# Experts' products issued by quarters of a matrix instead of whole matrices, and the first expert's low parts made on VectorE after the routing

## The chip, the cores and the metric

The kernel is one program on 1 core of a Trainium2 chip. Its time is device microseconds (us) of that core, given as the median of the runs. The engines are named as the profile names them: PE is TensorE (PEld its weight loads), DVE is VectorE, ACT is ScalarE, POOL is GpSimd and SP is SyncE, whose queue issues the large transfers.

## The reference, cut to what matters

The whole program is two blocks on 512 tokens of width 1024. The first is a state space mixer, an MLP, a sparse attention and another MLP. The second is an attention block followed by a mixture of 32 experts, and the change concerns this last layer alone. Each token goes to its 4 best experts. Every expert has three matrices of 1024 x 1024 in f32:

```python
logits = (h @ router_w + router_b).astype(jnp.float32)
top_logit, top_e = lax.top_k(logits, TOP_K)
top_w = jax.nn.softmax(top_logit, axis=-1)
...
gate = jnp.minimum(xe @ w_gate[e] + b_gate[e], SWIGLU_LIMIT)
up = jnp.clip(xe @ w_up[e] + b_up[e], -SWIGLU_LIMIT, SWIGLU_LIMIT)
act = (up + 1) * (gate * jax.nn.sigmoid(SWIGLU_ALPHA * gate))
return act @ w_down[e] + b_down[e]
```

A matrix is 4 MB, and all the experts' matrices together are 32 x 3 x 4 MB = 384 MB (of 1.0486 million bytes each), which have to be read once.

## The kernel before

**Routing.** `route` works out each token's weights, counts the tokens of each expert, sorts the experts by that count into ranks (`kr`, `gt`, `perm`), and stores the expert's number for each rank in `permi` and each token's place within its expert in `place`. `first` does the same ahead of that for rank 0, which is always the expert with number 0, and gathers its rows (`xy<-hx,gi`), so that this expert can start without the ranks. `route` also splits the three bias tables into a high and a low part (`b_gate`, `b_up`, `b_down`).

**Sizes of experts.** By rank an expert is computed in one of four ways. Ranks 1 to 3 (`HEAVY`) take two blocks of rows: 128 and 128 for rank 1, 128 and 64 for ranks 2 and 3. Ranks 0 and 4 to 10 take one block of 128 rows. Ranks 11 to 21 (`LIGHT`) take 64 rows and ranks 22 to 31 (`TINY`) take 32. The first eleven are called large below, the other 21 small.

**A quarter.** A matrix is read in four transfers of 1 MB on SP's queue (`fetch`, the tile `raw`). RAWS = 8 buffers hold them, and an issue waits until its buffer has been read out. For a large expert ACT rounds each half of a quarter to `wh` (L1772) and DVE subtracts that from `raw` to get `wl` (L1774), after which `raw` is free; then PE makes three products of 512 columns for each half and each half of the output (`mm3`, L170 to L172), 12 in a quarter. SPLITS buffers hold `wh`, as many `wl`. For expert 0 the low parts of the first two quarters are made on POOL, by the condition in L1774. For a small expert PE reads `raw` itself in f32 (L1804, `lac<-raw,xtf`), two or four column groups side by side, and `raw` is free once PE is through.

**The order.** `units` writes out a list of matrices (rank, t), t = 0 for gate, 1 for up, 2 for down. After expert 0, two matrices of small experts stand ahead of each matrix of a large one. `run` walks the list. In it `product` does all four quarters of a matrix, `after` the element-wise work behind it (L1860 to L1867), `act` transposes the gated rows for the third matrix (L1738, L1727), `table` finds an expert's rows (L1697, L1700), `gather` fetches them on POOL (L1713), and `start` transposes them. Tables are asked for five matrices ahead, gathers four. The function `ahead` splits the first two quarters of a large matrix before its turn. Within this order a scheduler moves single instructions, so that the matmuls of neighbouring pieces mix a little. The result of an expert is added to the output by an indirect DMA (L1890, `out_dram<-xy,si`).

Of the kernel before, what the change touches and what calls it, by code (L numbers as in the profile page):

```python
# [9 lines left out]
F32 = mybir.dt.float32  # L10
# [8 lines left out]
P = 128  # L19
NB = 4  # L20
# [1333 lines left out]
SPLITS = 5  # L1354
# [12 lines left out]
def units():  # L1367
# [25 lines left out]
class Moe:  # L1393
# [122 lines left out]
    def route(self):  # L1516
# [7 lines left out]
        self.bias = []  # L1524
        for n in ("b_gate_2", "b_up_2", "b_down_2"):
            raw = self.wp.tile([P, D], F32, name="bw", tag="wh")[:, :512]
            for i in range(4):
                nc.gpsimd.dma_start(raw[NE * i:NE * i + NE], a[n][0][:, i // 2 * 512:i // 2 * 512 + 512])
            x = bp.tile([P, 512], F32R, name=n)
            S.copy(x, raw)  # L1530
            for i in (1, 3):
                s = slice(NE * i, NE * i + NE)
                V.tensor_tensor(x[s], raw[s], x[s].bitcast(F32), op=OP.subtract)
            self.bias.append(x)
# [75 lines left out]
        V.tensor_copy(self.cnt, o)  # L1610

# [7 lines left out]
    def first(self, w4):  # L1619
# [24 lines left out]
        x0 = self.gather(gi)  # L1644
# [10 lines left out]
        self.xt0 = self.tiles(x0)  # L1655
# [33 lines left out]
    def table(self, r):  # L1689
# [5 lines left out]
        for i, slot in enumerate(todo):  # L1695
            oh = self.tp.tile([P, NB, P], F32R, name="ohs", bufs=1)
# [46 lines left out]
    def expert(self, e, xts, slots, es, out_rows, G=1):  # L1743
# [8 lines left out]
        early = bool(raws)  # L1752
# [13 lines left out]
        def split(t, c):  # L1766
            if (t, c) not in parts:
                raw = get(t, c)
                parts[t, c] = []
                for j in range(2):  # L1770
# [3 lines left out]
                    (G_ if early and t == 0 and c < 2 else V).tensor_tensor(wl, raw[:, j], wh.bitcast(F32), op=OP.subtract)  # L1774
                    parts[t, c].append((wh, wl))
            return parts[t, c]

        def ahead(t):
            if G == 1:
                for c in range(2):  # L1780
                    split(t, c)

        def act(t):

            if t == 2:
                st[2] = [self.tiles(u, G) for u in st["g"]]

        def grouped(t, mid):
            N, m = D // G, P // G
            ps = self.kk.ps.tile([P, 512], F32, name="lac", bufs=2)[:, :N]  # L1790
            b = self.bias[t]
            if G == 2:
                T.matmul(ps, pick[:, 0], b, start=True, stop=False)
            else:
                for i in range(2):
                    T.matmul(ps, pick[:, i], b[:, 256 * i:256 * i + 256], start=i == 0, stop=False)
# [371 lines left out]
```

## Time and profile before

| what | value |
|---|---|
| time, median of 3 runs | 2981.14 us (2977.97 to 2982.78) |
| the profiled execution's own time | 2984.59 us |
| its span in the trace | 2982.8 us, 38289 instructions |
| busy share of the span | PE 90%, PEld 67%, DVE 59%, ACT 40%, POOL 8% |
| moved between HBM and the core | 574.49 MB read, 21.53 MB written, 200 GB/s over the span |

Times in the rows below count from the start of the span. The experts' stage begins near 1841 us and lasts to the end. A busy PE in these rows is not PE at its peak, since the ends of matmuls are modelled; how fast it really goes is seen from the starts of successive matmuls.

### The profile page before, as it was taken

The page shows a single profiled execution, that of the slowest core. Times are in us where ns is not written, and L with a number is a line of the kernel's source. Part 1 is how long each engine was busy: PE and PEld are TensorE (multiplying, and loading weights), DVE is VectorE, ACT ScalarE, POOL GpSimd, SP SyncE. Part 2 cuts the span into 40 slices and gives each one's busy share as a digit, 9 for nine tenths or more (in the row PEclk, how much of TensorE's full clock was granted, in tenths as well). Part 3 has the DMA queues.
Part 4 walks back from the last instruction along what each step waited for, and adds up shares of the span by engine and source line. Part 5 has one row for each costly group of instructions (what it writes and reads, how often), then busy time and mean ns, then how long its engine had stood idle before and what let it go on. Part 6 is the DMA issues. An engine that isn't in the chain of part 4 may idle for free. (4 is left out here: it accounts for less than half of the span.)

```text
span 2982.8 us, 38289 instructions
## 1 busy us (share of the span) xinstructions
PE 2677.6 (90%) x14182; PEld 1996.0 (67%) x14182; DVE 1770.5 (59%) x3419; ACT 1191.8 (40%) x2208; POOL 245.2 (8%) x229
## 2 busy tenths in 40 slices
PE   5599999987999999899998997999989989988986
PEld 3488777886778888788888775556455455444553
DVE  6967565578874444589777558444444444444443
ACT  5353232454863333366655434332233232333232
POOL 3000000142000000200000002110110110110010
PEclk9799999998999999999999997999989999999997
DMA  3024454321023333211122555998999998999997
GB/s 116 15 99 176 150 197 156 94 60 54 29 93 127 96 96 99 93 50 41 53 60 72 181 198 203 385 361 358 349 353 363 342 357 353 350 359 376 381 406 295
DMA packets 193999, 595.95 MB, mean 200 GB/s; under 512 B 34960, under 2 KB 106056, under 8 KB 141320
## 3 DMA queue, kind: packets, MB, share of 16 engines
q1 hardware_dynamic: 179744, 564.33, 50.8%
q0 software_dynamic: 8752, 28.58, 3.4%
q8 instruction: 113, 1.85, 0.2%
q10 hardware_dynamic: 5312, 0.54, 0.1%
q14 instruction: 78, 0.64, 0.1%
HBM read 574.49 MB, written 21.53 MB: 200 GB/s over the span
## 5 line engine op out<-in xcount | busy, mean ns | idle before, releaser
L1804 PE MATMUL lac<-raw,xtf 128*32 128x256 f32 (+1 forms) x2976 | 378.6, 461 | 6.4 <-DMA raw<-in_w_down_dram 3.8
L152 DVE TENSOR_TENSOR wl<-wr,wh 128x1024 fp32r<-128x1024 f32 (+2 forms) x222 | 262.3, 1187 | 177.6 <-ACT wh L150 173.8
L150 ACT CAST wh<-wr 128x1024 fp32r<-128x1024 f32 (+2 forms) x228 | 228.8, 1008 | 295.4 <-PE acc L172 162.0
L1774 DVE TENSOR_TENSOR wl<-raw,wh 128x1024 fp32r<-128x1024 f32 x260 | 303.7, 1219 | 36.3 <-ACT wh L1772 35.2
L171 PE MATMUL wide<-wl,xth 128*128 128x512 f32 x576 | 259.8, 451 | 30.8 <-DVE wl L1774 30.6
L170 PE MATMUL wide<-wh,xth 128*128 128x512 f32 x576 | 256.1, 446 | 33.7 <-ACT wh L1772 32.4
L1772 ACT CAST wh<-raw 128x1024 fp32r<-128x1024 f32 x264 | 260.8, 1045 | 62.5 <-PE wide L172 37.0
L1804 PEld LDWEIGHTS lac<-raw,xtf 128*32 128x32 f32 (+1 forms) x2976 | 126.3, 119 | 193.8 <-issue 155.2
L170 PE MATMUL mm<-wh,xh 128*128 128x384 f32 (+2 forms) x664 | 230.1, 346 | 27.0 <-ACT gate L1264 12.8
L172 PE MATMUL wide<-wh,xtl 128*128 128x512 f32 x576 | 250.2, 434 | 0.0
L171 PE MATMUL mm<-wl,xh 128*128 128x384 f32 (+2 forms) x664 | 222.7, 335 | 3.1 <-DVE wl L152 2.9
L172 PE MATMUL mm<-wh,xl 128*128 128x384 f32 (+2 forms) x664 | 222.5, 335 | 1.2 <-DVE xl L166 1.2
L171 PE MATMUL acc<-wl,ffh 128*128 128x512 f32 x512 | 199.3, 389 | 0.7 <-DVE wl L152 0.7
L172 PE MATMUL acc<-wh,ffl 128*128 128x512 f32 x512 | 199.4, 390 | 0.0
L170 PE MATMUL acc<-wh,ffh 128*128 128x512 f32 x512 | 198.6, 390 | 0.0
L171 PEld LDWEIGHTS wide<-wl,xth 128*128 128x128 f32 x576 | 122.2, 212 | 99.4 <-DVE wl L1774 56.2
L170 PEld LDWEIGHTS wide<-wh,xth 128*128 128x128 f32 x576 | 121.3, 211 | 88.9 <-ACT wh L1772 46.6
L170 PEld LDWEIGHTS mm<-wh,xh 128*128 128x128 f32 x664 | 129.0, 194 | 44.1 <-ACT gate L1264 17.1
L172 PEld LDWEIGHTS wide<-wh,xtl 128*128 128x128 f32 x576 | 122.2, 212 | 34.7 <-issue 11.4
L171 PEld LDWEIGHTS mm<-wl,xh 128*128 128x128 f32 x664 | 129.0, 194 | 9.8 <-DVE wl L152 5.3
L172 PEld LDWEIGHTS mm<-wh,xl 128*128 128x128 f32 x664 | 129.2, 195 | 7.0 <-DVE xl L166 1.9
L1890 POOL DMA_INDIRECT out_dram<-xy,si x35 | 65.4, 1867 | 662.1 <-DVE xy L1889 482.2
(641 smaller groups left out, 5417.7 us busy)
## 6 DMA issues: line engine op xcount, KB each, us to landing
raw<-in_w_gate_dram SPq DMA_DIRECT2D x128, 1024.0 KB, 8.5
raw<-in_w_up_dram SPq DMA_DIRECT2D x128, 1024.0 KB, 11.4
raw<-in_w_down_dram SPq DMA_DIRECT2D x128, 1024.0 KB, 7.3
wr<-in_mlp_w_dram SPq DMA_DIRECT2D x128, 512.0 KB, 3.7
adaraw<-in_w_ada_dram SPq DMA_DIRECT2D x12, 2048.0 KB, 7.5
wr<-in_w_in_dram SPq DMA_DIRECT2D x16, 512.0 KB, 3.9
wr<-in_att_w_out_dram SPq DMA_DIRECT2D x12, 512.0 KB, 3.9
wr<-in_w_in_dram SPq DMA_DIRECT2D x48, 128.0 KB, 2.4
```

The source lines that it names most:

```text
L150: nc.scalar.copy(hi, raw)
L152: (eng or nc.vector).tensor_tensor(lo, raw, hi.bitcast(F32), op=OP.subtract)
L170: mmul(ps, ah, bh, start=first, stop=False)
L171: mmul(ps, ah, bl, start=False, stop=False)
L172: mmul(ps, al, bh, start=False, stop=last)
L1772: S.copy(wh, raw[:, j])
L1774: (G_ if early and t == 0 and c < 2 else V).tensor_tensor(wl, raw[:, j], wh.bitcast(F32), op=OP.subtract)
L1804: T.matmul(ps[m * g:m * g + m], x, raw[:, j, N * g:N * g + N], start=False, stop=c == 3 and j == 1)
L1890: G_.indirect_dma_start(out=out_rows, out_offset=bass.IndirectOffsetOnAxis(ap=si[:rows], axis=0), in_=y, in_offset=None, bounds_check=511, ...
```

## The change

The list holds quarters (rank, t, c) now (`steps`): expert 0's first six quarters stand alone, and from then on two quarters of small experts mostly follow each quarter of a large one. A large matrix's splits run one quarter ahead of its products. The hooks for table, gather and transposes sit at fixed distances in quarters: a table 16 ahead of an expert's first quarter, the gather 10, the transposes 8 for a large expert and 3 for a small one. The gated rows of a large expert are transposed two places ahead of its third matrix, which is behind two small quarters. The list of which expert follows which is unchanged, and so is the arithmetic but for the place of the bias products, which stand in a matrix's last quarter now. POOL no longer makes low parts. The rows of expert 0 and the bias tables are prepared at the end of `route`. SPLITS goes from 5 to 4, and the one-hot tile `ohs` has two buffers. The special early fetch of expert 0's third matrix is gone.

```diff
-SPLITS = 5
+SPLITS = 4
...
-    lane = iter(lane)
-    order = [(0, 0), (0, 1), next(lane), (0, 2)]
-    for u in [(r, t) for r in big[1:] for t in range(3)]:
-        order += [next(lane), next(lane), u]
+    lane = iter([(*u, c) for u in lane for c in range(4)])
+    order = []
+    for r in big:
+        gaps = [0] * 6 + [2, 2, 2, 2, 2, 0] if r == 0 else [2] * 7 + [4, 2, 2, 2, 0]
+        for (t, c), n in zip([(t, c) for t in range(3) for c in range(4)], gaps):
+            order += [(r, t, c)] + [x for _, x in zip(range(n), lane)]
     return order + list(lane)
...
         self.cnt = cp.tile([P, NE], F32, name="cnt")
         V.tensor_copy(self.cnt, o)
+        self.xt0 = self.tiles(self.x0)
+        for n, raw in zip(("b_gate_2", "b_up_2", "b_down_2"), raws):
+            x = bp.tile([P, 512], F32R, name=n)
+            S.copy(x, raw)
+            for i in (1, 3):
+                s = slice(NE * i, NE * i + NE)
+                V.tensor_tensor(x[s], raw[s], x[s].bitcast(F32), op=OP.subtract)
+            self.bias.append(x)
...
         def split(t, c):
-            if (t, c) not in parts:
+            if G == 1 and (t, c) not in parts:
                 raw = get(t, c)
...
-                    (G_ if early and t == 0 and c < 2 else V).tensor_tensor(wl, raw[:, j], wh.bitcast(F32), op=OP.subtract)
+                    V.tensor_tensor(wl, raw[:, j], wh.bitcast(F32), op=OP.subtract)
...
-            if early and t == 0:
-                raws.update(((2, c), self.fetch(e, (2, c))) for c in range(4))
...
+        n = 0
+        whole = [u for u in todo if groups(u[0]) == 1]
+        for p, (r, t, c) in enumerate(todo):
+            if r and t == c == 0:
+                n += 1
+                a = max(p - 16, n)
+                b = max(p - 10, a + 2)
+                at(a, table, r)
+                at(b, gather, r)
+                at(max(p - (8 if groups(r) == 1 else 3), b + 2), start, r)
+            if t == 2 and c == 0:
+                at(p - 2 if groups(r) == 1 else p - 3, lambda r: ex[r][1](), r)
         start(0)
...
+        ex[0][0](0, 0)
+        k = 0
+        for p, (r, t, c) in enumerate(todo):
+            for f in hooks.get(p, []):
+                f()
+            if groups(r) == 1 and (k := k + 1) < len(whole):
+                q, tq, cq = whole[k]
+                ex[q][0](tq, cq)
+            ex[r][2](t, c)
```

Where instructions stand is decided by the list and by the scheduler, so three places are shown as the built programs have them. The first is VectorE in the routing, from the one-hot rows of `first` (`w`, `ax`, weights of rank 0) and of all experts (`one`, `sw`) on. Before:

```order
L1550 TENSOR_TENSOR one<-one,w_16423 128x128
L1650 TENSOR_TENSOR ax_16441<-w_16464,ax_16441 128x4
L1551 TENSOR_REDUCE sw<-one 128x32
L1533 TENSOR_TENSOR b_up_16410<-bw,b_up_16410 32x512 x2
L1666 COPY sv_16474<-tr 128x4
L1551 TENSOR_REDUCE sw<-one 128x32
```

And after the change, from a few rows further up to the same reductions:

```order
L1553 SCALAR_TENSOR_TENSOR kc<-mm,c_keyc 128x1
L1778 TENSOR_TENSOR wl<-raw,wh 128x1024
L1647 TENSOR_SCALAR gi_16447<-tr 128x1
L1654 TENSOR_REDUCE w_16452<-w_16451 128x4
L1548 TENSOR_TENSOR one<-one,w_16411 128x128
L1655 CAST ax_16429<-w_16452 128x4
L1548 TENSOR_TENSOR one<-one,w_16411 128x128
L1656 TENSOR_TENSOR ax_16429<-w_16452,ax_16429 128x4
L1549 TENSOR_REDUCE sw<-one 128x32 x2
L1671 COPY sv_16462<-tr 128x4
```

The pair of `b_up` rows has moved from among the reductions to a place behind `perm`, and a first low part `wl` of expert 0, which was POOL's, stands on VectorE ahead of `gi`.

The second place is SyncE's queue behind the routing, where `TENSOR_LOAD permi` reads an expert's number and `ISA` are the checks on it. Before, three stretches of it:

```order
L1513 DMA hx<-nrm 128x1024 x4
L1429 DMA raw<-in_w_down_dram 128x2048 x2
L1904 TENSOR_LOAD permi
L1904 ISA x2
...
L1429 DMA raw<-in_w_gate_dram 128x2048
```

And after, where ten loads stand between the rows that are shown:

```order
L1516 DMA hx<-nrm 128x1024 x4
L1898 TENSOR_LOAD permi
L1898 ISA x2
...
L1432 ISA
L1432 DMA raw<-in_w_gate_dram 128x2048
L1432 ISA
L1432 DMA raw<-in_w_gate_dram 128x2048
L1432 DMA raw<-in_w_down_dram 128x2048
```

The two transfers of expert 0's third matrix that stood ahead of the loads are now mixed, one by one, with those of the small experts' quarters, and all of them are behind ten loads.

The third place is PE in the middle of the stage, around the transposes of the gated rows (`tr<-c_ident,gm`) of a large expert of one block, with tiny experts beside it. Before (24 rows of products of a large expert, L170 to L172, are left out in the middle):

```order
L1804 MATMUL lac<-raw,xtf 64x512 x12
L1793 MATMUL lac<-b_down_16419,pick 128x512
L1727 MATMUL tr<-c_ident,gl 128x128 x4
...
L1804 MATMUL lac<-raw,xtf 32x256 x16
L1738 MATMUL tr<-c_ident,gm 128x128 x8
L1727 MATMUL tr<-c_ident,xg 128x128 x2
```

And after the change:

```order
L172 MATMUL wide<-wh,xtl 128x512
L1796 MATMUL lac<-raw,xtf 32x256 x8
L1790 MATMUL lac<-b_up_16583,pick 128x256 x2
L1743 MATMUL tr<-c_ident,gm 128x128 x8
L1743 MATMUL tr<-c_ident,xy 128x128 x2
L170 MATMUL wide<-wh,xth 128x512
```

Where three quarters of a small expert (`x12`), two of a large one and two small ones stood in runs, single small quarters (`x8` of 256 columns, `x4` of 512) alternate with single large ones; between the large products and the transposes of `gm` stands one small quarter where there were two.

## Rows read from the trace of the kernel before

**Rows 1.** The page's 40 slices of the span, 74.6 us each: clock and transfers.

```profile
PEclk9799999998999999999999997999989999999997
...
GB/s 116 15 99 176 150 197 156 94 60 54 29 93 127 96 96 99 93 50 41 53 60 72 181 198 203 385 361 358 349 353 363 342 357 353 350 359 376 381 406 295
```

**Rows 2.** Busy times, clock and transfers by stretch; the first line names the columns.

```profile
core 0: us, PE busy (x) PEld busy (x) DVE busy (x) ACT busy (x) POOL busy (x), PEclk, DMA share, GB/s
1841.00:1900.00 59.00, 59.00 (x260) 34.67 (x259) 37.94 (x54) 26.46 (x32) 5.17 (x3) 1.00 0.99 394
1900.00:2700.00 800.00, 729.52 (x3794) 431.30 (x3793) 378.04 (x565) 244.24 (x340) 72.86 (x50) 0.93 0.92 355
...
2800.00:2960.00 160.00, 135.66 (x1008) 84.82 (x1004) 75.06 (x93) 53.70 (x76) 10.48 (x6) 0.90 1.01 410
1841.00:2960.00 1119.00, 1014.59 (x5465) 598.98 (x5463) 536.58 (x776) 352.42 (x483) 97.68 (x65) 0.93 0.94 366
```

**Rows 3.** What SP's queue waited for, 1841 to 2960 us: total, times, longest.

```profile
SPq L1429 <- PE lac L1804: 555.3, 238, 9.8
SPq L1429 <- DVE wl L1774: 280.1, 102, 6.4
```

**Rows 4.** Transfers of the stage: totals; issues by kind, with us to landing.

```profile
DMA packets 59813, 409.51 MB, mean 366 GB/s; under 512 B 7591, under 2 KB 7591, under 8 KB 12151
...
raw<-in_w_up_dram SPq DMA_DIRECT2D x124, 1024.0 KB, 11.0
raw<-in_w_down_dram SPq DMA_DIRECT2D x124, 1024.0 KB, 7.6
...
xy<-hx,gi POOLq DMA_INDIRECT x13, 9.3
```

**Rows 5.** PE's groups in the stage: count | busy us, mean ns | idle before.

```profile
L171 PE MATMUL wide<-wl,xth 128*128 128x512 f32 x561 | 253.1, 451 | 30.8 <-DVE wl L1774 30.6
L1804 PE MATMUL lac<-raw,xtf 128*64 128x512 f32 x1056 | 252.7, 600 | 0.0
L170 PE MATMUL wide<-wh,xth 128*128 128x512 f32 x560 | 248.6, 445 | 33.1 <-ACT wh L1772 32.4 <-ACT xth L165 0.6
...
L1804 PE MATMUL lac<-raw,xtf 128*32 128x256 f32 x1888 | 122.8, 383 | 1.3 <-DMA raw<-in_w_down_dram 1.3
```

**Rows 6.** PE in order of time, two successive products: start us, us.

```profile
1838.97 0.39 PE L172 MATMUL wide<-wh,xtl 128*128 128x512 f32 x1
1839.20 0.39 PE L170 MATMUL wide<-wh,xth 128*128 128x512 f32 x1
```

**Rows 7.** VectorE in order of time, in the routing: start us, us.

```profile
1799.87 0.68 DVE L1533 TENSOR_TENSOR b_gate<-bw,b_gate 32x512 fp32r<-32x512 f32 x1
...
1804.70 8.55 DVE L1533 TENSOR_TENSOR b_up<-bw,b_up 32x512 fp32r<-32x512 f32 x2
...
1815.23 1.61 DVE L1559 TENSOR_SCALAR perm<-c_iota,kc 128x32 f32<-128x32 f32 x1
...
1824.76 0.16 DVE L1580 CAST permi<-permf 1x32 int32<-1x32 f32 x1
```

**Rows 8.** POOL in order of time, in the routing.

```profile
1805.75 6.94 POOL L1774 TENSOR_TENSOR wl<-raw,wh 128x1024 fp32r<-128x1024 f32 x3
```

**Rows 9.** SP's queue in order of time, the first transfers past the eight.

```profile
1810.43 27.20 SPq L1429 DMA_DIRECT2D raw<-in_w_down_dram  x4
1841.09 10.34 SPq L1429 DMA_DIRECT2D raw<-in_w_gate_dram  x4
```

**Rows 10.** The loads of expert numbers on SP: duration ns min/median/max.

```profile
L1904 SPq TENSOR_LOAD <-permi x12: 261/268/463, 1825.0 to 1842.1; - x12
```

**Rows 11.** VectorE's groups in the stage.

```profile
L1774 DVE TENSOR_TENSOR wl<-raw,wh 128x1024 fp32r<-128x1024 f32 x255 | 297.6, 1219 | 33.6 <-ACT wh L1772 32.5
...
L1866 DVE TENSOR_SCALAR u<-wide 128x512 f32<-128x512 f32 x24 | 15.5, 686 | 42.9 <-PE wide L172 42.9
```

**Rows 12.** ACT's groups in the stage.

```profile
L1772 ACT CAST wh<-raw 128x1024 fp32r<-128x1024 f32 x253 | 249.6, 1045 | 41.5 <-PE wide L172 29.1 <-DMA raw<-in_w_up_dram 9.2 <-issue 2.0
```

More of the change, by code (lines that the diff above doesn't have):

```diff
@@ L1643, in first @@
         self.nx = self.ny = 0
-        x0 = self.gather(gi)
+        self.x0 = self.gather(gi)
         w = tp.tile([P, NB, 4], F32, name="w0")
@@ L1819, in product, with quarter @@
+        def quarter(t, c):
+            if G > 1:
+                grouped(t, c)
+            else:
+                if c == 0:
+                    st["p"] = [kk.wide() for _ in range(n)]
+                w = parts.pop((t, c))
+                for i, p in enumerate(st["p"]):
                     packed = st[0][i][0][1] is None
                     for h, hs in enumerate(halves):
-                        o = ps[i][:, hs]
+                        o = p[:, hs]
+                        if c == 3:
+                            m = 64 if packed else P
+                            T.matmul(o[:m], es[:, 2 * h + 1:2 * h + 2].to_broadcast([P, m]), self.bias[t], start=False, stop=False)
@@ L1829, in product @@
                                 kk.mm3(o, x[0], x[1], wh[:, hs], wl[:, hs], first, last)
-                            if first:
-                                m = 64 if packed else P
-                                T.matmul(o[:m], es[:, 2 * h + 1:2 * h + 2].to_broadcast([P, m]), self.bias[t], start=False, stop=False)
-                del parts[t, c]
-            st["p"] = [total(p, "gm" if t == 0 else "um") if st[0][i][0][1] is None else p for i, p in enumerate(ps)]
+            if c == 3:
+                st["p"] = [total(p, "gm" if t == 0 else "um") if st[0][i][0][1] is None and G == 1 else p
+                           for i, p in enumerate(st["p"])]
+                after(t)
         def total(p, name):
@@ L1901, in rows, with table, gather @@
             return 64 if i and r != HEAVY[0] else P
+        def table(r):
+            sl[r] = self.table(r)
+        def gather(r):
+            xs[r] = [self.gather(v[0], rows(r, k), groups(r)) for k, v in enumerate(sl[r])]
         def start(r):
@@ L2020, in overflow @@
                 V.tensor_copy(esr[:, 2 * i + 1:2 * i + 2], esf[:, i:i + 1])
-            ahead, act, product, after = self.expert(er, [xt], [v], esr, out_rows)
+            split, act, quarter = self.expert(er, [xt], [v], esr, out_rows)
             for t in range(3):
-                act(t)
-                product(t, lambda: None)
-                after(t)
+                if t == 2:
+                    act()
+                for c in range(4):
+                    split(t, c)
+                    quarter(t, c)
             V.tensor_scalar(cur[:, 0:1], cur[:, 0:1], 1.0, None, op0=OP.add)
```

112 lines of the change are left out of this document (24 added, 88 removed).

## The prediction

> **What bounds the kernel now.** I read the page's slices first. From the 26th slice to the end 15 slices in a row move 295 to 406 GB/s, while no slice before moves more than 203 [rows 1]. So the experts' stage is where transfers count, and the change lies in it and just ahead of it. Then I read the stage by stretches. From 1841 to 2960 us, 1119 us, it moves 409.51 MB [rows 4] at 366 GB/s; PE is busy 1014.59 us of it, at a granted clock of 0.93 [rows 2]. Neither is full. But the stretches differ: from 2800 to 2960 the transfers run at 410 GB/s, from 1841 to 1900 at 394 with PE busy all of the 59 us, and in the 800 us between 1900 and 2700 at 355 with PE idle for 70 us [rows 2]. The reader is to see that PE and the transfers wait for each other in turn, in the middle above all.
>
> Next, who holds the transfers back. SP's queue spends 555.3 us waiting for PE to release a buffer of a small expert and 280.1 us waiting for the low parts of a large one [rows 3], together 835 of the 1119 us. Waiting is what this queue should do when transfers are the bound; it hurts where too few are under way. In the other direction PE idles 30.8 us ahead of products with `wl` and 33.1 us ahead of those with `wh` [rows 5]. In the order of whole matrices a large one asks for four splits in a row. A quarter has 12 products, 0.23 us from start to start [rows 6], 2.76 us; VectorE needs 2 x 1.219 = 2.44 us for its two low parts, ACT 2 x 1.045 = 2.09 [rows 11, 12]. There is hardly slack, so every epilogue on VectorE makes PE late. Then eight small quarters follow in a row. Each takes PE 252.7 / 132 = 1.91 us with two groups or 122.8 / 118 = 1.04 us with four (a quarter's four or eight products stand as 8 or 16 rows, so 1056 rows are 132 quarters and 1888 are 118) [rows 5]. At 410 GB/s a megabyte takes 2.56 us, so PE eats up the eight buffers and waits.
>
> **The change part by part.** The start first. Before, the pair of `b_up` subtractions holds VectorE for 8.55 us, where one of the same form took 0.68 [rows 7]; POOL's three low parts run in the same time, 6.94 us [rows 8]. Without POOL's work the pair should take 1.4, so 7.2 us come off the chain to `permi`, which stands at 1824.76 [rows 7]: 1817.6. (`perm`, 1.61 us beside POOL's last part, may give another 1.4.) The first low part, now ahead of `gi`, and the one that stood behind it cancel. Then ten loads of numbers, 0.268 us each [rows 10] and checks that are not shown, stand ahead of all transfers behind the eight that are fetched before the stage; I put the first of those at 1821.5. Buffers come free at one a quarter of expert 0, 2.76 us, so the fifth transfer goes out at about 1832.5. Before, it went out at 1841.09, behind four that were spread over 27 us [rows 9]. That is 9 us gained; 14 if `perm` and the checks cost nothing, 4 if a quarter takes 4 us because VectorE (bias rows, tables and low parts in one queue) is late. Behind the fifth, 372 transfers are left in either kernel.
>
> The stage. The bytes, products, splits and epilogues are the same in number. What changes is the mix: 2.76 us of a large quarter and 2 x 1.91 = 3.82 or 2 x 1.04 = 2.08 of two small ones, against 3 x 2.56 = 7.7 us of transfers. So each group of three has less of PE's work than of the transfers', 6.6 or 4.8 us, with transposes and tables on top, and the split of the next large quarter has two or four small quarters and a large one, at least 2.76 + 2 x 2.08 = 6.9 us, to hide its 2.09 + 1.219 = 3.3 us. The 64 us of waiting for parts should vanish, and five to seven of eight buffers stay in flight.
>
> Bounds. Transfers alone, at the 410 GB/s of 2800 to 2960: 409.51 / 0.410 = 999 us. PE alone: its busy time of 1014.6 us at the clock of 0.93 would be 944 at the full clock. To PE are added new waits, since leads get shorter. The gated rows of a large expert were transposed behind two small quarters and are now behind one: four element-wise rows of 0.686 us [rows 11], 2.7 us, less 1.04 to 1.91, are 0.8 to 1.7 us for each of ten large experts. Their gathered rows are asked for two places, some 4 us, ahead of their transposes, and land in 9.3 us [rows 4]: up to 5 us each, 50 in all, if POOL issues them only there; nothing if it issues them when the table (six places earlier) is through. PE's upper bound is 1015 + 65 = 1080 us. Between 999 and 1080 I take the one stretch in which both ran without waiting: 1841 to 1900, PE busy all the time and 394 GB/s, so 409.51 / 0.394 = 1039 us. That is 80 us less than 1119.
>
> At no cost: the bias products only move within their matrix; four `wh` buffers hold the quarter in use and the next; the second `ohs` buffer lets a table start earlier. If the cover of the splits were gone, their price is the last rival's. The 22.8 us behind 2960 stay: a last quarter, epilogue and scatter.
>
> Sum: 2984.6 (the profiled execution) - 9 - 80 = 2895.6. That execution is 3.5 us above the median of the runs, so **2892 us**. With the bounds, -14 - 120 and -4 - 39, the likeliest case has 2847 to 2938.
>
> **Rivals.** First, PE becomes the bound through its clock. The clock was granted at 0.90, a mean of its two levels, in 2800 to 2960, where the transfers are dense and PE is busy 135.66 of 160 us, against 1.00 while PE was busy all the time [rows 2]. If short waits in every group of three keep it there, PE needs 944 / 0.90 = 1049 us, with all the new waits 1114: -5 - 9, 2967 us. The Trainium skill, "TensorE: Matmul & The Clock Gate", section "HAM oscillation", warns of just this: work per load that is shorter than the wait for the load makes the clock fall again and again. Against it: while transfers are the bound, a slower clock only eats waiting time, and a PE that falls behind has work queued and becomes dense again.
>
> Second, the stream is already at its bound and only the start is gained. Ten of the 15 slices lie between 342 and 363 GB/s [rows 1], which looks like a ceiling. Then -9: 2972 us. The Trainium skill, "HBM Reference", section "Specifications (TRN2)", gives about 358 GB/s as effective per core, and would put the ceiling there; the same section lets a core that streams alone go higher. The 410 over 160 us speaks against a ceiling.
>
> Third, slower: the split becomes the wait. Only one quarter is split ahead, and its buffers come free only when the quarter before the one in work is through. If VectorE has more than 3.6 us (6.9 - 3.3) of other rows in front of it, PE stands still, and the small quarters behind it hold their buffers. There are 132 such places. With PE's 1015 us this decides at (1119 + 9 - 1015) / 132 = 0.86 us at each; at 1.25 us the stage is 1180 us: +61 - 9, 3033 us. For it: an epilogue of two blocks has eight rows of 0.686, 5.5 us. Against it: that comes once in four quarters, for three experts.
>
> **How the numbers follow.** The forecast has 0.64, the clock 0.17, the ceiling 0.07, the splits 0.12. A measurement of this kernel can tell about 0.2%, 6 us, from no change. Faster by more: 0.64 and most of the clock's (0.13) and of the ceiling's (0.05), 0.82; same 0.06; slower 0.12. The range of 2850 to 2970 takes in the forecast's bounds but for their last microseconds, and the clock's case; it leaves out slower and a little on either side.
>
> **What would show it.** Right: `b_up` rows of 0.7 us, the fifth transfer of the stage at 1832, 390 GB/s or more in every 100 us behind it, PE's idle time ahead of `wh` and `wl` products down from 64 us to under 20. The clock's case would show PE busy over 95% with a granted clock at or under 0.90 and under 380 GB/s; the third, idle time ahead of L170 and L171 above 110 us; the second, 366 GB/s with more transfers under way, so landing times well above 7.6 and 11.0 us [rows 4]. A late gather would stand as idle time ahead of `tr<-c_ident,xy`. I would be wrong above all if PE's queue, which cannot pass a late piece, waits in places that I counted as covered.

## The result and the profile after

The changed kernel takes 3024.69 us (median of 4 runs, 3020.74 to 3030.89) against 2979.55 us (2977.29 to 2982.78) before: a ratio of 1.0153, with a 95% interval of 1.0129 to 1.0176. It is 45 us slower; the prediction had said 2892 us. The profiled execution has a span of 3019.3 us against 2982.8.

The page's slices of the span, 75.5 us each (they answer to [rows 1]):

```profile
PEclk9799999998999999999999989999899998999997
...
GB/s 114 15 106 180 157 188 152 88 54 49 29 102 129 98 98 98 83 52 36 50 51 91 264 126 351 356 365 314 352 369 313 341 369 292 332 352 357 390 401 235
```

The stretches of [rows 2], in the same columns, and in the last row the experts' stage from its first product of a large expert to its last of a small one. The clock in them is a mean of two levels, 0.50 (1.2 GHz) and 1.00 (2.4 GHz).

```profile
1841.00:1900.00 59.00, 56.90 (x239) 30.72 (x235) 29.23 (x54) 19.01 (x25) 3.42 (x2) 0.97 0.97 384
1900.00:2700.00 800.00, 717.43 (x3677) 391.58 (x3679) 360.76 (x545) 233.05 (x324) 103.59 (x49) 0.94 0.92 342
1841.00:2960.00 1119.00, 996.05 (x5192) 537.14 (x5188) 506.36 (x759) 331.87 (x459) 137.46 (x63) 0.94 0.94 353
...
1810.31:3000.25 1189.94, 1060.40 (x5553) 577.13 (x5553) 546.81 (x818) 358.39 (x492) 144.95 (x68) 0.94 0.92 348
```

and the same stage in the kernel before:

```profile
1826.27:2966.32 1140.05, 1032.38 (x5553) 612.04 (x5553) 547.58 (x811) 358.75 (x489) 101.51 (x68) 0.93 0.93 361
```

The reader is to see that the transfers got slower, not faster: 342 GB/s in the 800 us from 1900 where it was 355, and 353 in the whole of 1841 to 2960 where it was 366. PE's clock did not fall (0.94, before 0.93), but PE is idle for 1119 - 996 = 123 us, where it was 104. Over the whole stage PE is idle for 129.5 us instead of 107.7 and busy for 1060.4 instead of 1032.4.

What SP's queue waited for from 1841 to 2960 us, answering to [rows 3], is almost what it was:

```profile
SPq L1432 <- PE lac L1796: 553.9, 225, 5.8
SPq L1432 <- DVE wl L1778: 267.7, 70, 5.8
```

The transfers from 1841 to 3000 us, with the median time from issue to landing, answering to [rows 4]:

```profile
DMA packets 59160, 405.42 MB, mean 350 GB/s; under 512 B 7528, under 2 KB 7528, under 8 KB 11904
...
raw<-in_w_down_dram SPq DMA_DIRECT2D x125, 1024.0 KB, 7.8
raw<-in_w_up_dram SPq DMA_DIRECT2D x122, 1024.0 KB, 7.7
raw<-in_w_gate_dram SPq DMA_DIRECT2D x120, 1024.0 KB, 8.3
```

A quarter lands some 8 us after its issue; 350 GB/s times 8 us is an estimated 2.8 MB under way, of eight buffers of 1 MB. The other buffers are not empty: the queue waits for PE to release them. They hold quarters that have landed and lie there. So PE looks to be the bound, and the transfers follow it; a run with fewer buffers, below, bears it out.

PE's groups in the stage, answering to [rows 5] (there the window began at 1841 us, so that it held some products less):

```profile
L1796 PE MATMUL lac<-raw,xtf 128*64 128x512 f32 x1056 | 269.2, 628 | 0.0
L171 PE MATMUL wide<-wl,xth 128*128 128x512 f32 x576 | 259.2, 450 | 49.6 <-DVE wl L1778 49.6
L170 PE MATMUL wide<-wh,xth 128*128 128x512 f32 x576 | 251.4, 438 | 32.9 <-ACT wh L1776 24.9 <-DVE gm L1832 6.9 <-ACT pick L1764 0.6
...
L1796 PE MATMUL lac<-raw,xtf 128*32 128x256 f32 x1920 | 143.8, 424 | 0.0
...
L1743 PE MATMUL tr<-c_ident,gm 128*128 128x128 f32 x96 | 17.3, 315 | 12.9 <-DVE gm L1857 11.9 <-DVE xtl L166 0.4
```

Two things are to be seen. The idle time ahead of products with `wl` and `wh` (L171 and L170) is 82.5 us, 74.5 of them for these parts; it was 63.9 (63.0 for the parts) and should have vanished. And the small experts' products take longer, though their number is the same: 269.2 us against 252.7 with two groups, and 143.8 against 122.8 x 1920 / 1888 = 124.9 with four. That is 35 us that no step of the prediction had. Most of it turns out below to be the clock, whose low stretches now hold small products too.

The start went better than predicted. VectorE in the routing, answering to [rows 7]:

```profile
1803.77 0.68 DVE L1615 TENSOR_TENSOR b_up<-bw,b_up 32x512 fp32r<-32x512 f32 x1
...
1805.46 0.69 DVE L1615 TENSOR_TENSOR b_up<-bw,b_up 32x512 fp32r<-32x512 f32 x1
...
1807.93 0.16 DVE L1578 CAST permi<-permf 1x32 int32<-1x32 f32 x1
```

and SP's queue in order of time, its first five transfers, answering to [rows 9]:

```profile
1814.26 2.09 SPq L1432 DMA_DIRECT2D raw<-in_w_gate_dram  x2
1821.06 0.34 SPq L1432 DMA_DIRECT2D raw<-in_w_down_dram  x1
1824.40 3.40 SPq L1432 DMA_DIRECT2D raw<-in_w_gate_dram  x2
```

`permi` is there at 1807.93 us instead of 1824.76, 16.8 us earlier, and the fifth transfer has gone out by 1827.8 instead of 1841.09. Not all of this is the change's: the last logits of the routing (`lg`), ahead of anything that it touches, stand at 1793.73 us in this execution and at 1798.05 in the one before, and between 1789.5 and 1798.1 over all the runs of this document. From `lg` to `permi` it is 14.2 us instead of 26.7, so the change gives 12.5 us. All of the 16.8 us and more is lost behind `permi`: the span is 36.5 us longer, so that what lies behind `permi` takes 53 us longer.

### The profile page after: what moved, and what is told of

The parts are those of the page before. It is cut to its first block, busy times and chain, and to the rows that moved or that the text cites. A ratio compares the mean times of both kernels' runs of the same rounds, so it can differ in the third digit from the quotient of the medians.

```text
span 3019.3 us, 38279 instructions
## 1 busy us (share of the span) xinstructions
PE 2700.5 (89%) x14182; PEld 1957.5 (65%) x14182; DVE 1759.8 (58%) x3423; ACT 1190.7 (39%) x2208; POOL 279.5 (9%) x225
## 5 line engine op out<-in xcount | busy, mean ns | idle before, releaser
L1796 PE MATMUL lac<-raw,xtf 128*32 128x256 f32 (+1 forms) x2976 | 413.0, 496 | 0.0
L171 PE MATMUL wide<-wl,xth 128*128 128x512 f32 x576 | 259.2, 450 | 49.6 <-DVE wl L1778 49.6
L1776 ACT CAST wh<-raw 128x1024 fp32r<-128x1024 f32 x264 | 261.3, 1044 | 87.5 <-PE wide L172 78.5
L170 PE MATMUL wide<-wh,xth 128*128 128x512 f32 x576 | 251.4, 438 | 32.9 <-ACT wh L1776 24.9
L170 PE MATMUL mm<-wh,xh 128*128 128x384 f32 (+2 forms) x664 | 229.9, 346 | 26.0 <-ACT gate L1264 12.5
L172 PE MATMUL wide<-wh,xtl 128*128 128x512 f32 x576 | 241.3, 421 | 0.0
L171 PE MATMUL mm<-wl,xh 128*128 128x384 f32 (+2 forms) x664 | 222.7, 335 | 2.3 <-DVE wl L152 2.0
L172 PE MATMUL mm<-wh,xl 128*128 128x384 f32 (+2 forms) x664 | 222.6, 335 | 1.7 <-DVE xl L166 1.7
L171 PEld LDWEIGHTS wide<-wl,xth 128*128 128x128 f32 x576 | 115.9, 201 | 160.9 <-DVE wl L1778 80.0
L171 PE MATMUL acc<-wl,ffh 128*128 128x512 f32 x512 | 199.4, 389 | 0.8 <-DVE wl L152 0.8
L172 PE MATMUL acc<-wh,ffl 128*128 128x512 f32 x512 | 199.5, 390 | 0.0
L170 PE MATMUL acc<-wh,ffh 128*128 128x512 f32 x512 | 198.7, 390 | 0.0
L170 PEld LDWEIGHTS wide<-wh,xth 128*128 128x128 f32 x576 | 115.5, 201 | 100.0 <-issue 39.2
L1878 POOL DMA_INDIRECT out_dram<-xy,si x35 | 100.5, 2872 | 675.9 <-DVE xy L1877 475.7
L170 PEld LDWEIGHTS mm<-wh,xh 128*128 128x128 f32 x664 | 128.4, 193 | 43.0 <-ACT gate L1264 16.9
L172 PEld LDWEIGHTS wide<-wh,xtl 128*128 128x128 f32 x576 | 116.2, 202 | 41.6 <-issue 23.2
L171 PEld LDWEIGHTS mm<-wl,xh 128*128 128x128 f32 x664 | 128.3, 193 | 9.4 <-DVE wl L152 4.7
L172 PEld LDWEIGHTS mm<-wh,xl 128*128 128x128 f32 x664 | 128.6, 194 | 7.2 <-DVE xl L166 2.1
```

The lines of the kernel that those rows point to most:

```text
L170: mmul(ps, ah, bh, start=first, stop=False)
L171: mmul(ps, ah, bl, start=False, stop=False)
L172: mmul(ps, al, bh, start=False, stop=last)
L1776: S.copy(wh, raw[:, j])
L1796: T.matmul(ps[m * g:m * g + m], x, raw[:, j, N * g:N * g + N], start=False, stop=c == 3 and j == 1)
L1878: G_.indirect_dma_start(out=out_rows, out_offset=bass.IndirectOffsetOnAxis(ap=si[:rows], axis=0), in_=y, in_offset=None, bounds_check=511, ...
```

## Where PE's products stand

The change orders the work in a list: one quarter of a large expert, then two of small ones. The prediction reckoned with that list. But PE's instructions stand where the scheduler puts them. This is PE's list in the built program of the changed kernel, in the middle of the stage (`wide` are a large expert's products, `lac` a small one's, `tr<-aux,ohs` those of a table):

```
L1732 MATMUL tr_22084<-c_ident_64,gl_21820 128x128 x4
L1705 MATMUL tr_22097<-aux_15866,ohs_22098 128x4 x4
L170 MATMUL wide_21961<-wh_22010,xth_21579 128x512
L171 MATMUL wide_21961<-wl_22012,xth_21579 128x512
L172 MATMUL wide_21961<-wh_22010,xtl_21580 128x512
L170 MATMUL wide_21961<-wh_22014,xth_21579 128x512
L1796 MATMUL lac_22030<-raw_22032,xtf_21989 64x512 x4
L171 MATMUL wide_21961<-wl_22016,xth_21579 128x512
```

The small quarter `raw_22032` is listed ahead of the large quarter whose parts are `wh_22010` and `wl_22012`, and it stands behind that quarter's first four products. Counted over the stage, 109 of the 132 large quarters have their first product ahead of small quarters that are listed before them, mostly ahead of two (228 in all). And single small quarters stand inside large ones: PE goes 269 times from a large expert's products to a small one's, where the list has 116 such turns. In the kernel before it is 147 times, where the list of matrices has 32. These counts, which the experiments below go by, take in turns to a small expert's bias products (`lac<-b_up,pick`), which use the whole array like those of a large one (128*128 in the rows). Counted from a product over the whole array to one in column groups (`lac<-raw`), the programs have 245 changes, and 168 before.

PE's rows at such a place in the trace, in order of time (start us, us; the wait in brackets):

```profile
2743.90 0.59 PE L1705 MATMUL tr<-aux,ohs 128*128 128x4 f32 x4
2744.35 0.48 PE L170 MATMUL wide<-wh,xth 128*128 128x512 f32 x1
2745.88 0.50 PE L171 MATMUL wide<-wl,xth 128*128 128x512 f32 x1 [1.05 <-DVE wl L1778]
2746.22 0.40 PE L172 MATMUL wide<-wh,xtl 128*128 128x512 f32 x1
2746.46 0.39 PE L170 MATMUL wide<-wh,xth 128*128 128x512 f32 x1
2746.78 1.94 PE L1796 MATMUL lac<-raw,xtf 128*64 128x512 f32 x8
2748.64 0.50 PE L171 MATMUL wide<-wl,xth 128*128 128x512 f32 x1
2748.98 0.40 PE L172 MATMUL wide<-wh,xtl 128*128 128x512 f32 x1
2749.22 0.39 PE L170 MATMUL wide<-wh,xth 128*128 128x512 f32 x1
```

and VectorE's beside them:

```profile
2744.52 0.16 DVE L1671 COPY sv<-tr 128x4 f32<-128x4 f32 x1 [1.18 <-PE tr L1705]
2744.60 2.36 DVE L1778 TENSOR_TENSOR wl<-raw,wh 128x1024 fp32r<-128x1024 f32 x2
```

Here both costs are to be seen. First the wait: the low part stands in VectorE's queue behind `sv`, which needs the table's products on PE; so it starts at 2744.60, and PE, whose next product needs it, stands still for 1.05 us although a small quarter that needs nothing of VectorE stands three products further on in its queue. The cover of two small quarters, with which the prediction hid the split, stands behind the product that waits, not ahead of it. Second the change of kind: from one large product to the next it is 0.24 us, but 0.32 from the last one to `lac`, and 0.34 from the first one behind `lac` to the second.

## The experiments

Three theories stood at the beginning. A: PE is the bound, and each time it goes from products over the whole array (`wide`) to products in column groups (`lac`) and back it loses some 0.3 us. B: the pieces that VectorE and ACT make come late because leads got shorter. C, from the prediction: the transfers are the bound. Theory D came out of the first runs. The kernel before took 2978 to 2984 us beside the several groups of runs, so differences of a few us between groups are not read.

**The list's order on PE.** The one edit makes every product of a quarter stand behind the last product of the quarter listed before it. It is an edge of issue order on PE alone, but the scheduler, which goes by it, places rows of other engines anew: by the built programs' lists some 14% of VectorE's and 15% of ScalarE's stand otherwise than in the changed kernel.

```diff
-            ex[r][2](t, c)
+            with nullcontext() if p == 0 else self.kk.tc.issue_after(mm):
+                ex[r][2](t, c)
+            mm = [x for x in nc.cur_bb.bb.instructions[-200:] if x.engine == mybir.EngineType.PE][-1]
```

> The changed kernel with one edit: PE's products stand in the order of the list, so that both small quarters stand together between two large ones. In the changed kernel's instruction list PE goes 269 times from products of a large expert to those of a small one, in the kernel before 147 times, here 116 times. Theory A (each such change and the way back cost PE some 0.33 us, PE is the bound): (269 - 116) x 0.33 = 50 us less than the changed kernel, about 2974 us. Theory B (what was lost are pieces that come late, since leads got shorter): nothing is gained, and PE, which can no longer put other products ahead of a late piece, may lose some: 3020 to 3060 us. Theory C (the transfers are the bound and their order costs): no change, 3020 us.

Measured: 2860.12 us (2859.03 to 2862.81), against before a ratio of 0.9605 (0.9589 to 0.9621). That is 165 us less than the changed kernel, more than three times what theory A gave, and the opposite of B and C. The page's slices now show the transfers near 410 GB/s from the 27th to the 39th:

```profile
GB/s 121 15 89 171 138 208 184 71 89 63 16 30 170 103 96 96 94 90 47 31 60 53 84 196 191 260 409 410 407 381 411 405 410 414 393 414 418 414 415 274
```

The stage, in the columns of [rows 2]:

```profile
1809.65:2838.75 1029.10, 950.64 (x5553) 577.62 (x5553) 554.48 (x818) 365.76 (x492) 120.57 (x68) 0.98 1.00 402
```

PE's groups in it:

```profile
L1796 PE MATMUL lac<-raw,xtf 128*64 128x512 f32 x1056 | 251.4, 608 | 15.3 <-DMA raw<-in_w_down_dram 12.4 <-DMA raw<-in_w_gate_dram 1.7 <-DMA raw<-in_w_up_dram 1.1
L170 PE MATMUL wide<-wh,xth 128*128 128x512 f32 x576 | 240.1, 417 | 1.7 <-ACT s L1852 1.2 <-DVE cnt L1608 0.6
L171 PE MATMUL wide<-wl,xth 128*128 128x512 f32 x576 | 231.1, 401 | 2.6 <-DVE wl L1778 2.6
...
L1796 PE MATMUL lac<-raw,xtf 128*32 128x256 f32 x1920 | 130.8, 396 | 46.5 <-DMA raw<-in_w_down_dram 17.9 <-DMA raw<-in_w_up_dram 16.9 <-DMA raw<-in_w_gate_dram 11.1
```

and the landing times of its transfers from 1841 to 2838 us:

```profile
raw<-in_w_down_dram SPq DMA_DIRECT2D x125, 1024.0 KB, 16.9
raw<-in_w_gate_dram SPq DMA_DIRECT2D x120, 1024.0 KB, 18.3
```

The waits for parts are gone (82.5 us to 4.3), the clock is 0.98, and PE now waits for what the prediction wanted it to wait for, transfers: 61.8 us. Quarters land 17 to 18 us after their issue; at 402 GB/s that is an estimated 7 MB under way, nearly all the buffers. The stage takes 160.8 us less than the changed kernel's: PE is idle 51.1 us less (129.5 to 78.5) and busy 109.8 us less.

**The changes of kind, multiplied.** With the same order of quarters every large quarter is cut in four pieces and every small one in two, taken in turn; the core of the edit makes the products yield between pieces:

```diff
                 for g in range(G):
                     T.matmul(ps[m * g:m * g + m], x, raw[:, j, N * g:N * g + N], start=False, stop=c == 3 and j == 1)
+                yield
...
+            its = [gs[0], chain(*gs[1:])]
+            while its:
+                for g in list(its):
+                    with nullcontext() if mm is None else self.kk.tc.issue_after(mm):
+                        if next(g, its) is its:
+                            its.remove(g)
```

> The suspected cost multiplied: as the run with the list's order on PE, but every large quarter is cut in four pieces and every small one in two, which PE takes in turn. PE then goes 464 times from products of a large expert to those of a small one. Bytes, products, splits and the order of transfers stay. Theory A: (464 - 116) x 0.33 = 115 us more than the run with the list's order, about 3090 us; against the changed kernel 195 x 0.33 = 64 us more. Theory B: as the run with the list's order within 10 us, since the pieces are asked for at the same places. Theory C: no change against the changed kernel, 3020 us.

Measured: 2958.26 us (2955.79 to 2962.17), 98 us more than with whole quarters. In this run and in the next of its kind the transposes of a large expert's gated rows stand ahead of the multiplication by its up rows, so that the third matrix works on rows without that factor. The second run left whole the groups in which a large expert's second matrix ends:

> The list's order on PE with every large quarter cut in four pieces and every small one in two, taken in turn, but for the groups in which a large expert's second matrix ends, which are left whole; 431 changes of kind against 116. With 0.28 us each: 2860.1 + 315 x 0.28 = 2948 us; PE's idle time ahead of wl and wh stays under 10 us and its busy time grows by 315 x 0.33 = 104 us. If the changes cost nothing by themselves and the first fine run was slow from its order of transposes: 2860 to 2880 us.

Measured: 2948.15 us (2943.06 to 2952.74), just what 0.28 us a change gives. But that agreement was worth less than it looked: 25 us of PE's idle time in both runs stood ahead of transposes of gathered rows (`xy`), which are no part of the price of a change. A third run puts the transposes where they belong, behind the up rows, and moves them to the place of the third matrix's first quarter:

```diff
-                at(p - 2 if groups(r) == 1 else p - 3, lambda r: ex[r][1](), r)
+                at(p if groups(r) == 1 else p - 3, lambda r: ex[r][1](), r)
```

> The finely cut order once more (431 changes of kind), now with the transposes of a large expert's gated rows behind the multiplication by its up rows, which the two finely cut runs before left out of the third matrix. With 0.28 us a change 2948 us, and up to 8 us more for PE's waits for those rows; 2860 to 2880 us if the changes cost nothing.

Measured: 2916.64 us (2914.61 to 2920.02). The expectation missed by 31 us; some 22 of them are the waits for `xy`, which are 3.6 us here. Its stage and two of its groups (an added line of imports moves line numbers by one, so L171 is now the product with `wh` that opens a piece):

```profile
1811.41:2896.14 1084.73, 1044.64 (x5553) 523.61 (x5553) 552.33 (x817) 369.45 (x492) 110.40 (x67) 0.98 0.97 381
```

```profile
L171 PE MATMUL wide<-wh,xth 128*128 128x512 f32 x576 | 266.4, 463 | 5.0 <-ACT s L1858 4.2 <-DVE cnt L1609 0.6 <-ACT xth L166 0.2
...
L172 PE MATMUL wide<-wl,xth 128*128 128x512 f32 x576 | 229.4, 398 | 1.7 <-DVE wl L1779 1.7
```

At the same clock of 0.98, PE is busy 1044.64 - 950.64 = 94.0 us longer for 431 - 116 = 315 more changes, 0.30 us each; counted by the array it is 456 - 157 = 299 changes: **0.31 us each**. It shows where it should: in the product that opens a piece (463 ns, the others 398 to 400) and in the small experts' products. Of the 94 us only 56.5 come through in the time: PE's idle time in the stage falls from 78.5 us to 40.1, since the run with whole quarters had 62 us of waiting for transfers to take up the rest. Theory A's price is near. Its sum is not: counted by the array, 245 - 157 = 88 changes between the changed kernel and the list's order are 27 us of 165.

**Which products have to keep their place.** Theory D: what costs is that the next large quarter's products stand ahead of small ones that are ready. Two kernels force the order on one kind each:

```diff
-            with nullcontext() if p == 0 else self.kk.tc.issue_after(mm):
+            with nullcontext() if p == 0 or groups(r) > 1 else self.kk.tc.issue_after(mm):
```

> The changed kernel with the list's order forced on PE for large quarters alone: none of their products may stand ahead of the small quarters listed before them; the small ones may still go ahead. Theory D (what costs is that PE's list puts products of the next large quarter ahead of small ones that are ready, so that they stand at the head of PE's queue and wait for their parts; PE then idles and its clock falls; the changes of kind come on top with some 0.28 us each, (2958.26 - 2860.12) / (464 - 116) of the two runs that differ in them): as with the whole list's order, 2860 us, and PE's idle time ahead of products with wl and wh under 10 us (here are 119 changes). Theory A (the changes alone): 3024.7 - (269 - 119) x 0.33 = 2975 us. If it is the small quarters' place that matters: 3020 us.

Measured: 2864.01 us (2862.58 to 2866.06); the idle time ahead of L170 and L171 is 2.2 us. The counterpart has `groups(r) == 1` in the same place:

> The counterpart: the list's order forced on PE for small quarters alone; large ones may still go ahead of small ones listed before them (265 changes). Theory D: as the changed kernel, 3000 to 3030 us, with 70 us or more of idle time ahead of products with wl and wh. If it is the small quarters' place that matters: 2860 us.

Measured: 3028.02 us (3021.93 to 3029.88), as the changed kernel. Its groups:

```profile
L171 PE MATMUL wide<-wl,xth 128*128 128x512 f32 x576 | 261.9, 455 | 52.5 <-DVE wl L1778 52.5
...
L170 PE MATMUL wide<-wh,xth 128*128 128x512 f32 x576 | 251.6, 438 | 53.8 <-ACT wh L1776 45.5
```

In the list of the first no large quarter stands ahead of a small one listed before it, in that of the second 109 do. Holding the large quarters' products in place is what gives the gain; the small ones need no edge of their own. How much of it comes through PE's own order, and how much through the rows of VectorE and ScalarE that move with it, was not separated; where the edge left those rows nearly as they were (the counterpart), nothing was gained.

**More lead instead of another order.** If the waits come from late parts, asking for them earlier should help as well:

```diff
-SPLITS = 4
+SPLITS = 6
...
-                q, tq, cq = whole[k]
-                ex[q][0](tq, cq)
+                for q, tq, cq in whole[k:k + 2]:
+                    if q in ex:
+                        ex[q][0](tq, cq)
```

> The changed kernel with PE's order left to the scheduler (268 changes), but the parts of a large quarter asked for two large quarters ahead instead of one, with six buffers for each kind of part instead of four; to make room, seven buffers for loaded quarters instead of eight and one for one-hot rows instead of two. Theory D: the waits for wl and wh (74 us in the changed kernel) go, with them most of the time at half clock, and only the changes' cost stays: 2860 + 152 x 0.28 = 2903 us; if half of the waits stay, 2960. Theory A (changes alone, leads play no part): 3020 us.

Measured: 3082.64 us (3079.43 to 3095.16), 58 us slower than the changed kernel and far from every expectation. The waits stay:

```profile
L171 PE MATMUL wide<-wl,xth 128*128 128x512 f32 x576 | 266.4, 463 | 59.9 <-DVE wl L1778 59.8
...
L170 PE MATMUL wide<-wh,xth 128*128 128x512 f32 x576 | 257.0, 448 | 36.6 <-ACT wh L1776 27.1
```

PE's list tells why the lead is gone: the large quarters' first products have moved forward with their parts, now ahead of 459 small quarters listed before them, mostly four, where it were 228. As far as these lists show, a part that is asked for earlier only brings an earlier product. Three sizes changed in this run along with the lead, so how its 58 us divide was not tried.

**Are turns by quarters needed?** Two kernels keep the list's order on PE and make the turns coarser, two and four, then four and eight quarters (whole matrices, as before the change):

```diff
-        gaps = [0] * 6 + [2, 2, 2, 2, 2, 0] if r == 0 else [2] * 7 + [4, 2, 2, 2, 0]
+        gaps = [0] * 7 + [4, 0, 4, 0, 2] if r == 0 else [0, 4] * 6
```

> The changed kernel with the list's order on PE and coarser turns: two quarters of a large expert, then four of small ones. PE goes 63 times from large to small. Theory A: (269 - 63) x 0.33 = 68 us less than the changed kernel, about 2957 us, and 17 us less than the run with turns of one and two. Theory B: two large quarters in a row ask for their splits with less cover, so about as the run with turns of one and two or up to 20 us slower. Theory C: no change, 3020 us.

Measured: 2861.94 us (2858.22 to 2864.22). The second has `[0] * 7 + [4, 0, 0, 0, 6]` and `[0, 0, 0, 8] * 3`:

> The list's order on PE, but in turns of whole matrices as before the change: four quarters of a large expert, then eight of small ones (32 changes of kind; tables, gathers and starts asked for four places earlier, as the longer turns need). Theory D: it is PE's order and not the quarters that gives the 118 us against the kernel before; with the transfers the bound at 410 GB/s as in the runs of 2860 us, 2855 to 2885 us. Theory E (the turns by quarters are needed as well, because four splits in a row, 4 x 2 x 1.22 = 9.8 us on VectorE against 4 x 2.76 = 11.0 us of products, have no cover when an epilogue comes between): waits for wl and wh of 30 us and more, 2900 to 2960 us.

Measured: 2869.99 us (2869.40 to 2873.45). With turns of one and two, two and four, and four and eight quarters the time is 2860, 2862 and 2870 us. Of the price of a change these runs say little, for counted by the array they have 157, 157 and 134 changes. But whole matrices lose no more than 10 us: once PE keeps the list's order, the turns by quarters, which the prediction thought worth 80 us, are worth 10. With whole matrices in that order the time is 109 us below the kernel before, of which the new start, below, gives 8.

**The start alone.** The kernel before, with only the low parts moved to VectorE and the bias rows and expert 0's transposes moved behind the ranks:

> The kernel before with only the new start: expert 0's low parts all on VectorE, and the bias rows and expert 0's transposes behind the ranks. The order of the experts' work stays that of whole matrices (148 changes on PE). All theories: the 16 us that the changed kernel gained ahead of its first large product (1826.27 to 1810.31) come through, 2979 - 16 = 2963 us. If instead the start's gain is eaten up later by waiting for transfers (theory C), 2979 us, no change.

Measured: 2969.70 us (2964.84 to 2974.93), a ratio of 0.9969 (0.9959 to 0.9980): 8 us in the medians, 13.6 in the profiled executions (2982.8 to 2969.2), of the 16 expected. But 4.3 of those 16 stood ahead of the routing and are no gain of the change, and the profiled execution of the kernel before was one of its slower ones; by the medians the start gives about two thirds of the rest.

**Buffers.** Six for loaded quarters instead of eight, once with the list's order and once in the changed kernel:

```diff
-RAWS = 8
+RAWS = 6
```

> The run with the list's order on PE (2860 us), with six buffers for loaded quarters instead of eight. There the transfers are the bound: a quarter lands 17 to 18 us after its issue. If all eight buffers are needed for that, every buffer less costs: with two fewer 2890 to 2930 us; if six are enough for 410 GB/s, 2860 us.

Measured: 2884.94 us (2882.91 to 2886.18), 25 us more than with eight.

> The changed kernel, PE's order left to the scheduler, with six buffers for loaded quarters instead of eight. The prediction took the transfers for a bound beside PE, so that two buffers fewer would cost 5% and more of the stage (3070 us and more). Theory D: in the changed kernel quarters land 8 us after their issue and then lie waiting for PE, so two of the eight buffers only hold what waits: 3025 us, within 15 us.

Measured: 3029.43 us (3011.05 to 3031.95), which can't be told from the 3024.69 with eight. Two buffers that cost 25 us where the transfers are the bound cost nothing that can be seen in the changed kernel. That settles theory C for it.

## Why the prediction was wrong, by its steps

**What bounds the kernel.** "PE and the transfers wait for each other in turn" was misread. SP's 835 us of waiting [rows 3] were read as a sign that the transfers are near their bound; they were full buffers behind a late PE. Two rows pointed there: the small experts' products wait only 1.3 us for transfers [rows 5], and quarters land in 7.6 to 11.0 us [rows 4], where it is 17 to 18 with nearly all buffers under way. The changed kernel has 8, and does as well with six buffers; the kernel before was not run with fewer.

**The split's cover: the step that failed.** That the split of the next large quarter "has two or four small quarters and a large one" to hide its 3.3 us took the list for the order on PE. In 109 of 132 places small quarters stood behind the product that they were to cover for. (The 6.9 us also count four small quarters; with the two that the sentence names as well, the cover is 4.8 us, and 1.5 us of slack are left instead of 3.6.) So "The 64 us of waiting for parts should vanish" became 82.5, and with it fell the term of -80 us. With the list's order forced (first run) what that step said comes true: 4.3 us of waiting, and 402 GB/s over the stage where 394 had been taken. 2860 us lie 32 below the prediction, within its range.

**The term that was missing.** "The bytes, products, splits and epilogues are the same in number" is right, but products cost more when the array's division changes between them. The changed kernel has 245 - 168 = 77 such changes more, at 0.31 us some 24 us, which the prediction put at nothing. The Trainium skill has the rule, in "TensorEngine Tiling (Array Packing)", section "Key Properties": a change of tiling mode drains the engine. The rows agree, with 0.31 us for each change. It spoke against this change, and the prediction did not weigh it.

**Why it is slower than before, then.** Of the 53 us behind `permi`, 49.9 are in the stage: 21.9 more of idle time and 28.0 more of PE's busy time. The 77 changes are some 24 of the 28. The clock is hardly a part of it, for the stage has 152 us at the lower level and had 157. But its low stretches now hold small products too: by the traces' records of the clock, 58 us of their busy time are at 0.50, where it was 2 us before, and 80 us of the busy time of the products with `wh` and `wl`, where it was 135. The same 16 rows of a small quarter show it, 1.07 us at the full clock and 1.93 at half of it behind two waits:

```profile
2924.62 1.07 PE L1796 MATMUL lac<-raw,xtf 128*32 128x256 f32 x16
2927.31 0.51 PE L1790 MATMUL lac<-b_gate,pick 128*128 128x256 f32 x2 [1.62 <-ACT s L1876]
2929.68 0.80 PE L170 MATMUL wide<-wh,xth 128*128 128x512 f32 x1 [1.86 <-ACT wh L1776]
...
2932.09 1.93 PE L1796 MATMUL lac<-raw,xtf 128*32 128x256 f32 x16
```

```profile
2928.20:2935.00 6.80, 4.86 (x22) 2.23 (x23) 5.78 (x6) 4.27 (x5) 1.55 (x1) 0.50 0.96 363
```

By that ratio the clock is an estimated (58 - 2) x (1 - 1.07 / 1.93) = 25 of the 35 us on the small products, and the large ones have about as much back. Against the list's order the changed kernel's stage has 160.8 us to lose: 51 of idle time, 88 x 0.31 = 27 of changes, and by the mean clock of 0.94 against 0.98 some (1060 - 27) x (1 - 0.94 / 0.98) = 42. About 40 us of PE's busy time are left unassigned. Part of them belongs to the waits themselves: the product behind a wait shows 0.50 us instead of 0.39 too (2745.88 in the rows above).

**The start** was right in its mechanism and too small to `permi`: 12.5 us instead of 7.2, with 4.3 more by the luck of the execution. The `b_up` rows took 0.7 us as forecast; `perm` took 0.23 instead of 1.61, the 1.4 that the prediction had in brackets, and the `b_down` pair (1.4 us) moved behind `permi`. In the time the new start alone gives 8 us, where 9 had been forecast.

**The new waits** were of the right size: 12.9 us ahead of the transposes of `gm` where 8 to 17 were forecast. The 50 us for late gathers were not needed: the 1.9 us ahead of the transposes of `xy` were not for a gather.

**The rivals.** The clock's did not happen (0.94 against 0.93). The ceiling's is refuted: 402 GB/s over the stage in the first run, where the second rival had 366. The Trainium skill's 358 GB/s per core ("HBM Reference", section "Specifications (TRN2)") is no ceiling for one core alone, as the same section says, and the 402 GB/s agree. The third, splits as the wait, named the right place and came nearest with 3033 us, but that was in part luck: it put the wait down to other rows in front on VectorE and decided at 110 us of idle time ahead of L170 and L171. There were 82.5, and with PE's 1015 us these would have made the stage shorter than before; the rest of the loss came from PE's longer busy time.

**The clock as a consequence.** The clock was 0.98 with 40 us of idle time in a stage of 431 turns, 0.94 in the changed kernel with 130, and 0.90 in the run with more lead, whose stage from 1812.25 to 3069.70 us holds 161 (row below). The Trainium skill warns, in "TensorE: Matmul & The Clock Gate", section "HAM oscillation", that waits between bursts of work pull the clock down; these runs agree.

```profile
1812.25:3069.70 1257.45, 1096.58 (x5553) 594.61 (x5553) 550.58 (x818) 355.30 (x490) 110.38 (x67) 0.90 0.89 330
```

The changes of kind do not lower it. The sum of the idle time does not fix it: the runs with whole quarters and with whole matrices in the list's order have 78 and 80 us, most of it waiting for transfers, at 0.98 and 0.95. That each of the waits lowers the clock by itself was read off the rows, not tried.

## What to carry to other kernels

A list that orders work is not the order on an engine: before reckoning with a cover, look in the built program whether the covering instructions stand ahead of the one that waits. If they don't, force the place of the instruction that waits; here an edge of issue order for the large quarters alone turned a loss of 45 us into a gain of some 115. Time from issue to landing told here which side was the bound better than a queue's waiting time or a rate: landings of 8 us with full buffers went with a late consumer, and two of the eight buffers then gave nothing that could be seen.

## What the runs showed of the hardware

Going from full-array products to products in column groups and back cost TensorE 0.31 us of busy time each time at a clock of 0.98. The starts of successive rows in the third finely cut run, medians where the clock was full, show where: 0.33 us instead of 0.23 from the last `wide` to the first `lac`, 0.52 instead of 0.42 (two groups) or 0.31 instead of 0.20 (four) from the last `lac` to the first `wide`, and 0.34 instead of 0.23 behind the first `wide`. The DMA engines' busy share says little of how much they could still do: it was 0.92 at 348 GB/s with an estimated 2.8 MB under way, and 1.00 at 402 GB/s. And subtractions of 32 rows on VectorE that took 8.55 us for two beside POOL's subtractions [rows 7] took 0.68 and 0.69 us without them.
